# A planner's clock with other prices: transfers at 280 bytes per ns, table loads left out

## The chip, the cores and the metric

The kernel runs on one core of a Trainium2 chip. The metric is the device time of one execution in microseconds (us), less is better. Before the change three runs took 842.88, 843.17 and 847.2 us, a median of 843.17 us. Five engines work beside each other, each through its own queue in the order in which the program gave it the instructions: TensorE (PE, matrix products and transposes), VectorE (DVE), ScalarE (ACT), GpSimd (POOL) and SyncE (SP, which only issues DMA transfers here).

## The reference

Two layers of an encoder over 256 tokens of width 1024, all in fp32:

```python
h = rms_norm(x, norm_mix_g)
rq, rk, rv, rg, pv, nq, nk, nv, mq = split(h @ w_in, 9)      # each 256 wide
ret  = rms_norm(retention(rotary(rq), rotary(rk), rv)) * silu(rg)
pool = multiscale_pool(pv, pool_w, pool_scale)               # windows 2, 4, 8, 16
na   = neighbourhood_attention(norm(nq), norm(nk), nv, rpb)
mk, mv = split(rms_norm(mem, norm_mem_g) @ w_mem_kv, 2)      # 256 memory tokens
mo   = memory_attention(norm(mq), norm(mk), mv)
up   = einsum('bsnc,ncd->bsnd', stack([ret, pool, na, mo]), w_branch)
x    = x + sum(sigmoid(h @ w_gate) * up) @ w_out
a, g = split(rms_norm(x, norm_ffn_g) @ w_ffn_in, 2)          # 2816 wide each
x    = x + (silu(a) * g) @ w_ffn_out
```

Every branch has 4 heads of 64. The weights are 136 MB of the two layers together, read once.

## The kernel before, in words

**Weights.** The 256 tokens are two tiles `t` of 128. All weights pass through 272 slots of 128x1024 fp32 (512 KB), in a fixed order: 136 slots a layer (0 to 135, 136 to 271). A slot comes by DMA into one of four buffers `raw`; ACT copies it, rounded, to one of ten buffers `whi` (`split_hi`, a CAST in the profile); DVE subtracts that from `raw` into one of ten `wlo` (`split_lo`) and then issues the next transfer (`issue_dmas`). The two together are called the casts of a slot. TensorE multiplies with both halves: three products for each fp32 product (`whi` by the high half of the activation, `wlo` by its high half, `whi` by its low half), 12 matmuls of 512 columns a slot, into the PSUM banks A0 to A3 or B0, B1. Slots 0 to 17 of a layer are `w_in`; then come, branch by branch, the gates, the memory's keys and values (slots 22 to 25) and the branch projections; 62 to 69 are `w_out`, 70 to 135 the FFN.

**Small work.** Everything else is written as Python generators (chains): the evacuation of a bank, norms, softmax (`attention`, buffers `sc`), transposes through banks C0 and C1, retention, pooling (`branch_chain`), the FFN's hidden units (`hid_chain`, `hid_T`, buffers `w0` to `w3`), the gates (`gate_chain`, buffer `gt`).

**The planner.** No hand wrote the order on the queues. While the program is written out, a planning clock (`Clock`, L66) keeps a time for each engine and for the DMA: `enter` takes every instruction, `cost` prices it, and a tile's last write and read are noted with the time that comes out. All decisions ask `soon(t)`: is `t` at most a little past the time to which TensorE has been planned? `pump` puts the casts of the next slot into the ACT and DVE queues as soon as the clock says that the raw transfer has landed, the buffer is free and the engine's queue is not planned further ahead than `WINDOW` allows; `background` takes the next step of each chain that is due; the main loop then takes the next group of matmuls. So a price is never executed, but it decides which of two instructions stands first in a queue, and each engine then keeps that order on the chip whatever really lands first. A wrong price cannot give a wrong result: the semaphores follow from the order.

The transfer's price is in `enter`: SP is held 0.45 us, the data start 1.2 us after that at the earliest, pass at 390 bytes per ns (512 KB: 1.34 us) one after the other, and count as landed 1.0 us later. A switch of ACT's function table between exponential and sigmoid costs TABLE_LOAD. The instruction itself (ACT_TABLE_LOAD) is put in by the compiler wherever two activations that follow one another need different tables.

Of the kernel before, what the change touches and what calls it, by code (L numbers as in the profile page):

```python
# [9 lines left out]
F32 = mybir.dt.float32  # L10
F32R = mybir.dt.float32r
AF = mybir.ActivationFunctionType
# [11 lines left out]
HD = 64  # L24
# [9 lines left out]
LEAD = 7  # L34
MAX_LAG = 8
WARM = 6.6
TABLE_LOAD = 1.28
WINDOW = (6, 4, 1.5, 0.4)
VERBOSE = False
BRANCHES = (2, 3, 0, 1)  # L40
# [3 lines left out]
class Engine:  # L44


    def __init__(self, real, clock, name):
        self.real, self.clock, self.name = real, clock, name

    def __getattr__(self, op):  # L50
        f = getattr(self.real, op)

        def call(*args, **kw):
            outs = [kw[k] for k in ("out", "accum_out") if kw.get(k) is not None]
            ins = [v for k, v in kw.items() if k not in ("out", "accum_out")]
            rest = list(args)
            if "out" not in kw:
                outs.append(rest.pop(0))
            func = next((v for v in rest if isinstance(v, AF)), None)
            self.clock.enter(self.name, op, outs, [v for v in ins + rest if isinstance(v, bass.AP)], kw, func)  # L60
            return f(*args, **kw)  # L61

        return call


class Clock:  # L66
# [5 lines left out]
    def __init__(self):  # L72
        self.at = dict.fromkeys(("PE", "ACT", "DVE", "POOL", "SP", "DMA"), 0.6)
        self.reads, self.writes = {}, {}
        self.mark = 0.0
        self.column = None
        self.narrow = False
        self.table = None

    @property  # L80
    def now(self):
# [2 lines left out]
    def cost(self, eng, op, outs, ins, kw):  # L84
        n = max([x.free_size() for x in outs[-1:] + ins[:1]])
        if eng == "PE":
            o = outs[0]
            n = o.free_size() * (2 if self.now < WARM else 1)
            narrow = op == "matmul" and ins[0].dtype == F32 and o.partition_size() == HD
            change = 0.2 * (narrow != self.narrow)  # L90
            self.narrow = narrow
            if op == "transpose":
                return n * 0.845e-3 + change
            if ins[0].dtype == F32R:
                return n * 0.4167e-3 + 0.0135 + change
            half = o.partition_size() == HD and o.base_partition()
            if o.partition_size() == HD:
                pair, self.column = self.column, None if half else n
                if half and pair == n:
                    return 0.02  # L100
            return max(n, 128) * 1.67e-3 + change
        if eng == "ACT":
            return 0.1 + n * 0.83e-3 + 0.1 * (kw.get("accum_out") is not None) + 0.04 * isinstance(kw.get("scale"), bass.AP)
        if eng == "POOL":
            if op == "memset":
                return 0.1 + n * 1e-3
            return 0.3 + 0.17 * n
        if op in ("tensor_copy", "tensor_scalar", "tensor_scalar_mul", "tensor_scalar_add", "memset"):
            return 0.085 + n * 0.6e-3
        return 0.08 + n * 1.045e-3 + 0.05 * (op == "scalar_tensor_tensor")  # L110

    def span(self, x):
        (stride, parts), *free = x.ap
# [12 lines left out]
        old = [r for r in table.get(key, ()) if r[4] > end - 60 and not (p0 <= r[0] and r[1] <= p1 and lo <= r[2] and r[3] <= hi)]  # L126
        table[key] = old + [(p0, p1, lo, hi, end, eng)]

    def enter(self, eng, op, outs, ins, kw, func=None):
        ins = [x for x in ins if x.space != bass.MemoryType.DRAM]  # L130
        outs = [x for x in outs if x.space != bass.MemoryType.DRAM]
        skip = "PE" if eng == "PE" else None
        t = max([self.last(self.writes, x) + self.LATENCY for x in ins]
                + [self.last(self.reads, x, eng) + self.LATENCY for x in ins if x.space == bass.MemoryType.PSUM]
                + [max(self.last(self.writes, x, skip), self.last(self.reads, x, skip)) + self.LATENCY for x in outs] + [self.at[eng]])
        if func in (AF.Exp, AF.Sigmoid) and func != self.table:
            self.table = func
            self.at["ACT"] += TABLE_LOAD
            t = max(t, self.at["ACT"])
        if op == "dma_start":  # L140
            self.at[eng] = t + 0.45
            t = max(self.at["DMA"], t + 1.2) + (outs + ins)[0].nbytes() / 390e3
            self.at["DMA"] = t
            end = t + 1.0
        else:
            end = self.at[eng] = t + self.cost(eng, op, outs, ins, kw)
        for x in ins:
            self.note(self.reads, x, end, eng)
        for x in outs:
            self.note(self.writes, x, end, eng)  # L150
        self.mark = max(self.mark, end)
# [1030 lines left out]
```

## Time and profile before

| | |
|---|---|
| three runs | 842.88, 843.17, 847.2 us (median 843.17) |
| profiled execution | 841.89 us, its span 840.0 us |
| granted clock of TensorE | 1.000 of full speed (2.4 GHz) |
| PE busy | 820.8 us (98%), 3928 instructions |
| DVE, ACT busy | 552.2 us (66%), 470.1 us (56%) |
| DMA | 152.86 MB, mean 182 GB/s |
| chain that ended last | PE 78%, ACT 7%, DMA 7%, DVE 6%, issue 2% |

How to read it: all recorded instructions carry one line, L61, the helper through which every operation goes, so groups are told apart by the names of their tiles (written out<-in). Times in a timeline are microseconds from the start of the span. A timeline's row gives start, duration, engine, line, operation, tiles, shape, how many instructions it joins (x8), and in brackets how long the engine was idle before it and what released it. The end of a matmul is modelled: successive matmuls overlap, so the step from start to start is what a matmul costs.

### The profile page before, as it was taken

How to read it: one execution, taken by the hardware profiler on the slowest of the kernel's cores; microseconds unless marked ns; L12 is line 12 of the kernel's file. 1: busy time of each engine (PE TensorE's matmuls, PEld its weight loads, DVE VectorE, ACT ScalarE, POOL GpSimd, SP SyncE). 2: the span in 40 equal slices, each digit the busy share in tenths (PEclk: the TensorE clock that was granted, in tenths of full speed). 3: DMA queues.
4: the chain of work that ended last, by engine and by line, in shares of the span. 5: the costliest groups of instructions: out<-in, count | busy, mean ns of one | idle time of the engine just before them, and what ended most of it. 6: DMA issues, size and time to landing. Idle time of an engine off the chain costs nothing.

```text
span 840.0 us, 10795 instructions
## 1 busy us (share of the span) xinstructions
PE 820.8 (98%) x3928; PEld 672.4 (80%) x3928; DVE 552.2 (66%) x802; ACT 470.1 (56%) x726; POOL 30.5 (4%) x32
## 2 busy tenths in 40 slices
PE   8999999999999999999999998999999999999998
PEld 6788778778887888888888877887888878888886
DVE  5898786865677556555568868584775765655541
ACT  6858887445465444444469677754444654444430
POOL 0400100000000000000011001000000000000000
PEclk9999999999999999999999999999999999999999
DMA  8946765546568656566374477446544676666611
GB/s 257 323 140 203 240 199 166 166 147 197 176 180 255 191 180 197 176 198 185 95 220 137 156 246 219 147 126 226 178 157 120 200 228 198 187 187 186 189 52 51
DMA packets 103765, 152.86 MB, mean 182 GB/s; under 512 B 6432, under 2 KB 55328, under 8 KB 103712
## 3 DMA queue, kind: packets, MB, share of 16 engines
q1 hardware_dynamic: 102848, 151.30, 57.1%
q10 hardware_dynamic: 864, 0.88, 0.3%
q8 instruction: 31, 0.51, 0.2%
q14 instruction: 22, 0.18, 0.1%
HBM read 151.10 MB, written 1.05 MB: 181 GB/s over the span
## 4 chain that ended last, share of the span: by engine, by line
PE 78%; ACT 7%; DMA 7%; DVE 6%; issue 2%; POOL 0%; SPq 0%; DVEq 0%; ACTq 0%; POOLq 0%
PE A L61 49%; PE B L61 25%; PE C L61 4%; DVE wlo L61 3%; ACT whi L61 2%; DMA raw<-in_w_in 2%; DMA mem<-in_pool_a 2%; DMA raw<-in_w_ffn_out 1%; DMA raw<-in_w_gate 1%; DVE w L61 1%; ACT rs L61 1%; ACT sc L61 1%; DMA raw<-in_w_mem_kv 1%; ACT qk L61 1%; ACT bhi L61 1%
## 5 line engine op out<-in xcount | busy, mean ns | idle before, releaser
L61 DVE TENSOR_TENSOR wlo<-raw,whi 128x1024 fp32r<-128x1024 f32 (+1 forms) x275 | 330.2, 1212 | 190.9 <-ACT whi L61 190.3
L61 ACT CAST whi<-raw 128x1024 fp32r<-128x1024 f32 (+1 forms) x273 | 284.1, 1050 | 214.0 <-PE A L61 83.0
L61 PE MATMUL A<-whi,hhi 128*128 128x512 f32 (+1 forms) x544 | 213.9, 393 | 1.6 <-ACT whi L61 0.7
L61 PE MATMUL A<-wlo,hhi 128*128 128x512 f32 (+1 forms) x544 | 208.9, 384 | 1.0 <-DVE wlo L61 1.0
L61 PE MATMUL A<-whi,hlo 128*128 128x512 f32 (+1 forms) x544 | 209.1, 384 | 0.0
L61 PEld LDWEIGHTS A<-whi,hhi 128*128 128x128 f32 x544 | 102.3, 188 | 23.2 <-issue 2.6
L61 PEld LDWEIGHTS A<-whi,hlo 128*128 128x128 f32 x544 | 102.2, 188 | 21.2 <-DVE hlo L61 0.8
L61 PEld LDWEIGHTS A<-wlo,hhi 128*128 128x128 f32 x544 | 102.5, 188 | 20.1 <-DVE wlo L61 2.0
L61 PE MATMUL B<-whi,hlo 128*128 128x512 f32 x288 | 112.5, 391 | 0.1
L61 PE MATMUL B<-whi,hhi 128*128 128x512 f32 x288 | 112.3, 390 | 0.0
L61 PE MATMUL B<-wlo,hhi 128*128 128x512 f32 x288 | 112.1, 389 | 0.0
L61 PE MATMUL A<-whi,bhi 128*128 128x512 f32 x272 | 108.3, 398 | 0.0
L61 PE MATMUL A<-whi,blo 128*128 128x512 f32 x272 | 106.2, 390 | 0.0
L61 PE MATMUL A<-wlo,bhi 128*128 128x512 f32 x272 | 106.1, 390 | 0.0
L61 PEld LDWEIGHTS B<-whi,hlo 128*128 128x128 f32 x288 | 54.0, 188 | 12.9 <-DVE hlo L61 1.8
L61 PEld LDWEIGHTS B<-wlo,hhi 128*128 128x128 f32 x288 | 54.1, 188 | 11.3
L61 PEld LDWEIGHTS B<-whi,hhi 128*128 128x128 f32 x288 | 54.1, 188 | 11.0
L61 PEld LDWEIGHTS A<-whi,blo 128*128 128x128 f32 x272 | 51.1, 188 | 11.0
L61 PEld LDWEIGHTS A<-whi,bhi 128*128 128x128 f32 x272 | 51.1, 188 | 10.4 <-issue 0.8
L61 PEld LDWEIGHTS A<-wlo,bhi 128*128 128x128 f32 x272 | 51.2, 188 | 9.7
L61 DVE SCALAR_TENSOR_TENSOR w<-B,rms,w 128x256 f32<-128x256 f32 x72 | 34.7, 482 | 3.9 <-ACT w L61 2.6
L61 ACT CAST bhi<-C 128x512 fp32r<-128x512 f32 x28 | 16.4, 586 | 34.4 <-PE C L61 34.3
(115 smaller groups left out, 605.5 us busy)
## 6 DMA issues: line engine op xcount, KB each, us to landing
raw<-in_w_ffn_in SPq DMA_DIRECT2D x176, 256.0 KB, 3.2
raw<-in_w_gate SPq DMA_DIRECT2D x64, 512.0 KB, 4.4
raw<-in_w_ffn_out SPq DMA_DIRECT2D x44, 512.0 KB, 3.9
raw<-in_w_in SPq DMA_DIRECT2D x35, 512.0 KB, 4.3
raw<-in_w_branch SPq DMA_DIRECT2D x16, 512.0 KB, 4.5
raw<-in_w_out SPq DMA_DIRECT2D x16, 512.0 KB, 4.2
raw<-in_w_mem_kv SPq DMA_DIRECT2D x8, 512.0 KB, 4.3
xn<-in_bias SPq DMA_DIRECT2D x4, 512.0 KB, 5.4
```

Of the source, the lines that this page charges most:

```text
L61: return f(*args, **kw)
```

## The change

Only the prices of the planning clock change. Of a transfer: SP is held 0.48 us in place of 0.45, the data start 1.1 us later in place of 1.2, pass at 280 bytes per ns in place of 390 (512 KB: 1.87 us in place of 1.34), and count as landed 0.9 us later in place of 1.0. A switch of ACT's table costs the clock nothing any more (`TABLE_LOAD` and the `func` that was handed along are gone), nor does a change between matmuls of 64 and of 128 rows of output (`narrow`, 0.2 us). A transpose, an fp32r matmul (512 columns: 0.216 us in place of 0.227) and DVE's operations get slightly different prices.

```diff
-TABLE_LOAD = 1.28
...
-            narrow = op == "matmul" and ins[0].dtype == F32 and o.partition_size() == HD
-            change = 0.2 * (narrow != self.narrow)
-            self.narrow = narrow
             if op == "transpose":
-                return n * 0.845e-3 + change
+                return n * 0.84e-3
             if ins[0].dtype == F32R:
-                return n * 0.4167e-3 + 0.0135 + change
+                return n * 0.416e-3 + 0.003
...
-            return max(n, 128) * 1.67e-3 + change
+            return max(n, 128) * 1.67e-3
...
-            return 0.085 + n * 0.6e-3
-        return 0.08 + n * 1.045e-3 + 0.05 * (op == "scalar_tensor_tensor")
+            return 0.07 + n * 0.55e-3
+        return 0.07 + n * 1.05e-3 + 0.05 * (op == "scalar_tensor_tensor")
...
-        if func in (AF.Exp, AF.Sigmoid) and func != self.table:
-            self.table = func
-            self.at["ACT"] += TABLE_LOAD
-            t = max(t, self.at["ACT"])
         if op == "dma_start":
-            self.at[eng] = t + 0.45
-            t = max(self.at["DMA"], t + 1.2) + (outs + ins)[0].nbytes() / 390e3
+            self.at[eng] = t + 0.48
+            t = max(self.at["DMA"], t + 1.1) + (outs + ins)[0].nbytes() / 280e3
             self.at["DMA"] = t
-            end = t + 1.0
+            end = t + 0.9
```

The queues hold the same instructions as before, but for ACT_TABLE_LOAD: 12 in place of 10, both new ones in the second softmax of layer 0. Their order differs in the mixers (the part of a layer ahead of its FFN) of both layers and in the first blocks of each FFN; from the fourth block on the FFN's order is the same. On SP five raw transfers trade places with the bias, memory or norm tables beside them; on POOL one power in layer 0 moves ahead of two others. Both stay put otherwise, `pool_a` included.

The ACT queue in the first blocks of the FFN of layer 0, before (`whi` are casts of slots, `w3<-A2` the sigmoid of the first block's second tile, `bhi` the cast of transposed hidden units):

```order
L61 CAST whi5_78<-raw1_70 128x1024
L61 CAST whi6_79<-raw2_71 128x1024
L61 ACTIVATE w3_128<-A2_63,rms_136 128x256
L61 CAST whi7_80<-raw3_72 128x1024
L61 CAST whi8_81<-raw0_69 128x1024
L61 CAST bhi1_98<-C1_68 128x512
```

and now:

```order
L59 CAST bhi0_97<-C0_67 128x512
L59 CAST whi5_78<-raw1_70 128x1024
L59 ACTIVATE w3_128<-A2_63,rms_136 128x256
L59 CAST whi6_79<-raw2_71 128x1024
L59 CAST whi7_80<-raw3_72 128x1024
L59 CAST bhi1_98<-C1_68 128x512
```

The sigmoid stands ahead of the cast of slot 86 (`whi6`), where it stood behind it; the same trade is made in layer 1 with slot 222. In layer 1 the evacuation of the second tile of memory keys (`w3<-A2`) likewise moves ahead of the casts of slots 169 and 170, which stood ahead of it.

The ACT queue in the second softmax of layer 0, before (`sc0`, `sc1` with `sums` are exponentials, without it the scaling of their rows, `gt` the sigmoids of the first gates, `mem0` the retention's decay):

```order
L61 CAST whi5_78<-raw1_70 128x1024
L61 ACTIVATE sc0_119,sums0_151<-sc0_119,sums0_151 128x256 x2
L61 ACTIVATE sc1_120,sums1_152<-sc1_120,sums1_152 128x256 x2
L61 ACTIVATE mem0_123<-mem0_123 128x512
L61 ACTIVATE sc0_119<-sc0_119,sums0_151 128x256
L61 CAST whi6_79<-raw2_71 128x1024
L61 ACTIVATE sc1_120<-sc1_120,sums1_152 128x256
L61 ACT_TABLE_LOAD
L61 ACTIVATE gt_109<-A1_62,rms_136 128x512
L61 ACTIVATE gt_109<-A3_64,rms_136 128x512
L61 COPY sc0_119<-B0_65 128x512
L61 ACT_TABLE_LOAD
```

and now:

```order
L59 CAST whi5_78<-raw1_70 128x1024
L59 ACT_TABLE_LOAD
L59 ACTIVATE gt_109<-A1_62,rms_136 128x512
L59 CAST whi6_79<-raw2_71 128x1024
L59 ACT_TABLE_LOAD
L59 ACTIVATE sc0_119,sums0_151<-sc0_119,sums0_151 128x256 x2
L59 ACT_TABLE_LOAD
L59 ACTIVATE gt_109<-A3_64,rms_136 128x512
L59 ACT_TABLE_LOAD
L59 ACTIVATE sc1_120,sums1_152<-sc1_120,sums1_152 128x256 x2
L59 ACTIVATE mem0_123<-dist_150,lg_134 128x512
L59 ACTIVATE sc1_120<-sc1_120,sums1_152 128x256
```

The gates' sigmoids now stand between the exponentials, and a table load at every change from one to the other.

The TensorE queue in the pooling of layer 1, before (`B0<-mem0`, `mem1` are the pooling's products, whose `mem` tiles come by the transfer `pool_a`; the rows ahead are matmuls of slots 183 and 184):

```order
L61 MATMUL A3_64<-whi3_76,hhi1_94 128x512
L61 MATMUL A3_64<-wlo3_86,hhi1_94 128x512
L61 MATMUL A3_64<-whi3_76,hlo1_96 128x512
L61 MATMUL B0_65<-mem0_123,qk4_115 64x136 x2
L61 MATMUL B0_65<-mem0_123,qk4_115 64x16 x2
L61 MATMUL B0_65<-mem0_123,qk4_115 64x120 x2
L61 MATMUL B0_65<-mem1_124,qk4_115 64x136 x2
L61 MATMUL B0_65<-mem1_124,qk4_115 64x16 x2
L61 MATMUL B0_65<-mem1_124,qk4_115 64x120 x2
L61 MATMUL A1_62<-whi4_77,hhi0_93 128x512
L61 MATMUL A1_62<-wlo4_87,hhi0_93 128x512
L61 MATMUL A1_62<-whi4_77,hlo0_95 128x512
```

and now:

```order
L59 MATMUL A3_64<-whi4_77,hhi1_94 128x512
L59 MATMUL A3_64<-wlo4_87,hhi1_94 128x512
L59 MATMUL A3_64<-whi4_77,hlo1_96 128x512
L59 MATMUL A1_62<-whi5_78,hhi0_93 128x512
L59 MATMUL A1_62<-wlo5_88,hhi0_93 128x512
L59 MATMUL A1_62<-whi5_78,hlo0_95 128x512
L59 MATMUL B0_65<-mem0_123,qk4_115 64x136 x2
L59 MATMUL B0_65<-mem0_123,qk4_115 64x16 x2
L59 MATMUL B0_65<-mem0_123,qk4_115 64x120 x2
L59 MATMUL B0_65<-mem1_124,qk4_115 64x136 x2
L59 MATMUL B0_65<-mem1_124,qk4_115 64x16 x2
L59 MATMUL B0_65<-mem1_124,qk4_115 64x120 x2
```

The products stand 15 matmuls later, behind slot 184 and a quarter of slot 185; in layer 0 they stand 3 rows later than before.

## Rows read from the trace of the kernel before

**Rows 1.** The page's first part: busy time, share of the span and instructions by engine.

```profile
PE 820.8 (98%) x3928; PEld 672.4 (80%) x3928; DVE 552.2 (66%) x802; ACT 470.1 (56%) x726; POOL 30.5 (4%) x32
```

**Rows 2.** TensorE's waits: who waited for what, us in total, times, longest.

```profile
PE C L61 <- DVE w L61: 7.6, 5, 3.0
...
PE B L61 <- DMA mem<-in_pool_a: 1.8, 3, 1.1
```

**Rows 3.** Timeline of TensorE, layer 0 to 46 us and layer 1 from 440 us.

```profile
36.50 1.09 PE L61 MATMUL C<-ident_gain,w 128*128 128x128 f32 x8 [1.58 <-DVE blo L61]
...
45.69 0.66 PE L61 MATMUL C<-ident_gain,mem 128*128 128x128 f32 x4 [0.23 <-DVE blo L61]
...
440.65 0.39 PE L61 MATMUL A<-wlo,hhi 128*128 128x512 f32 x1
440.87 0.39 PE L61 MATMUL A<-whi,hlo 128*128 128x512 f32 x1
441.41 0.66 PE L61 MATMUL C<-ident_gain,mem 128*128 128x128 f32 x4
...
470.52 0.50 PE L61 MATMUL A<-wlo,hhi 128*128 128x512 f32 x1 [0.52 <-DVE wlo L61]
```

**Rows 4.** Timeline of TensorE, its other waits.

```profile
100.08 0.30 PE L61 MATMUL C<-ident_gain,w 128*128 128x128 f32 x1 [1.32 <-DVE w L61]
...
113.61 0.50 PE L61 MATMUL A<-whi,hhi 128*128 128x512 f32 x1 [0.64 <-DVE xn L61]
...
263.01 0.55 PE L61 MATMUL C<-ident_gain,w 128*128 128x128 f32 x3 [1.68 <-DVE w L61]
...
514.73 0.52 PE L61 MATMUL C<-ident_gain,w 128*128 128x128 f32 x3 [2.99 <-DVE w L61]
...
582.63 0.78 PE L61 MATMUL B<-mem,qk 128*64 128x136 f32 x12 [1.08 <-DMA mem<-in_pool_a]
...
676.94 0.55 PE L61 MATMUL C<-ident_gain,w 128*128 128x128 f32 x3 [0.96 <-DVE w L61]
```

**Rows 5.** Timeline of ACT and VectorE at the first FFN block of each layer.

```profile
259.74 1.05 ACT L61 CAST whi<-raw 128x1024 fp32r<-128x1024 f32 x1 [1.66 <-DMA raw<-in_w_ffn_out]
...
261.96 1.00 DVE L61 SCALAR_TENSOR_TENSOR w<-A,rms,w 128x256 f32<-128x256 f32 x2
...
673.66 1.05 ACT L61 CAST whi<-raw 128x1024 fp32r<-128x1024 f32 x1 [0.76 <-DMA raw<-in_w_ffn_out]
```

**Rows 6.** Timeline of ACT and GpSimd at the memory keys of layer 1.

```profile
505.56 1.05 ACT L61 CAST whi<-raw 128x1024 fp32r<-128x1024 f32 x1 [1.63 <-PE A L61]
...
507.24 1.05 ACT L61 CAST whi<-raw 128x1024 fp32r<-128x1024 f32 x1
...
509.02 0.49 ACT L61 ACTIVATE w<-A,rms 128x256 f32<-128x256 f32 x1
...
511.93 1.86 POOL L61 TENSOR_TENSOR sm<-sm,mhalf 128x4 f32<-128x4 f32 x1 [1.50 <-DVE sm L61]
```

**Rows 7.** Issue of the pooling tables in layer 1, and their time to landing.

```profile
576.01 0.82 SPq L61 DMA_DIRECT2D mem<-in_pool_a  x2
...
DMA to landing us min/median/max: 6.6/7.0/7.4
```

**Rows 8.** Timeline of ACT and TensorE at the second softmax of layer 0.

```profile
79.84 0.50 ACT L61 ACTIVATE sc<-sc,sums 128x256 f32<-128x256 f32 x1
80.36 1.28 ACT L61 ACT_TABLE_LOAD   x1
81.66 1.27 ACT L61 ACTIVATE gt<-A,rms 128x512 f32<-128x512 f32 x2
...
81.99 0.60 PE L61 MATMUL B<-ident_gain,sc 128*128 128x128 f32 x4
```

**Rows 9.** Timeline of VectorE and TensorE at slots 14 and 15 of layer 0.

```profile
52.31 2.35 DVE L61 TENSOR_TENSOR wlo<-raw,whi 128x1024 fp32r<-128x1024 f32 x2
...
54.39 0.39 PE L61 MATMUL A<-wlo,hhi 128*128 128x512 f32 x1
```

More of the change, by code (lines that the diff above doesn't have):

```diff
@@ L58, in call @@
                 outs.append(rest.pop(0))
-            func = next((v for v in rest if isinstance(v, AF)), None)
-            self.clock.enter(self.name, op, outs, [v for v in ins + rest if isinstance(v, bass.AP)], kw, func)
+            self.clock.enter(self.name, op, outs, [v for v in ins + rest if isinstance(v, bass.AP)], kw)
             return f(*args, **kw)
@@ L76, in __init__ @@
         self.column = None
-        self.narrow = False
-        self.table = None
     @property
@@ L127, in note, with enter @@
         table[key] = old + [(p0, p1, lo, hi, end, eng)]
-    def enter(self, eng, op, outs, ins, kw, func=None):
+    def enter(self, eng, op, outs, ins, kw):
         ins = [x for x in ins if x.space != bass.MemoryType.DRAM]
```

## The prediction

> **What bounds the kernel now.** I read the page's first part, then TensorE's waits, then each wait in the timeline with the queues it hangs on. TensorE is busy 820.8 of 840 us [rows 1], so the change can win little more than its waits. The table of waits shows where most are: 7.6 us in five waits of bank C for a `w` tile that VectorE writes, and 1.8 us in three waits for the pooling's tables [rows 2]. The timeline shows that all sit where small work (softmax, norms, hidden units) hands something to TensorE, none in the FFN's middle [rows 3, 4].
>
> A wait costs slightly more than its bracket says. A matmul of 512 columns is shown 0.39 us long, but the next starts 0.22 us after it [rows 3]; so a pause is the bracket plus some 0.16 us of refill. The wait before 36.50 costs 1.58 + 0.16 = 1.74, that at 514.73 costs 2.99 + 0.16 = 3.15. Where no bracket is shown, the step says it: from 440.87 to 441.41 is 0.54, of which 0.23 is the matmul and 0.31 a pause [rows 3].
>
> **What the change does.** It changes the order alone. With a slower transfer the clock believes that raw weights land later, so `pump` offers a cast later and small work gets ahead of it. That cuts both ways: small work comes sooner where a cast stood before it, and the cast comes later where its slot was just in time. No matmul, cast or byte is added; of instructions only two table loads, 1.28 us each on ACT [rows 8]. The slightly shorter prices of TensorE and VectorE bring no term of their own; what they do is in the order already. Terms, from the order as it now stands and durations of the trace:
>
> 1. **FFN starts.** The sigmoid of the first block's second tile stands ahead of the cast it stood behind. That cast waited for its transfer, ACT idle 1.66 us before 259.74 and 0.76 before 673.66 [rows 5], then took 1.05. VectorE could multiply only at 261.96, and TensorE's transposes stood until 263.01. In the new order the sigmoid doesn't wait for a landing, and with 2.7 us and 1.8 us gained (idle plus cast) both waits are gone: (1.68 + 0.16) + (0.96 + 0.16) = **-2.96** [rows 4, 5]. The cast that now stands later has its matmuls some slots away; its cover is the ring of ten buffers. Bounds: -2.96, and 0 if VectorE is late for another reason.
>
> 2. **Memory keys of layer 1.** The evacuation at 509.02 stood behind two casts, at 505.56 and 507.24, each some 0.95 from start to start; ACT was idle 1.63 before the first [rows 6]. Both go behind it: 1.9 sooner, and I count 0.4 of the idle time, as the first tile's evacuation is still ahead. The power on GpSimd, 1.86 us each [rows 6], remains, and the chain over it. The wait of 3.15 [rows 4] falls by **-2.3**. Bounds: 0 (the first power is late and holds the second) and -3.15.
>
> 3. **Pooling.** SP issues the tables at 576.01 and they land 6.6 to 7.4 us later [rows 7]; their place among the transfers is unchanged. The products that wait for them move 15 matmuls later in layer 1, 15 x 0.227 = 3.4 us of other work, against a wait of 1.08 + 0.16 and a smaller one behind it; in layer 0 by three rows, 0.7 us against its one. The three waits sum to 1.8 + 3 x 0.16 = 2.3 [rows 2, 4]: **-2.3**. What is late next is the pooled branch's projection, which the planner gives a slot's distance. Bounds: -2.3, and 0 if the transfer itself slips as far as the products, since its neighbours on SP are raw transfers that wait for casts.
>
> 4. **Gate products at 113.61**, held by VectorE's merging: 0.64 + 0.16 = **-0.8** [rows 4]; the sums now stand ahead of a cast. Bounds: -0.8 and 0.
>
> 5. **Start of layer 1**: 0.31 at 441.41 and 0.52 + 0.16 at 470.52 [rows 3]. The latter is a slot whose `wlo` is just late. Small work around it is reordered and the slot before it comes in sooner: **-1.0**. Bounds: -1.0, and +2.0 if more small work stands before that cast.
>
> 6. **Layer 0 up to 66 us.** Two waits go: 1.74 and 0.23 + 0.16, together -2.1 [rows 3]. But here weights are just in time: the first of the two subtractions from 52.31 (2.35 for both, so it ends near 53.5) is used at 54.39, a slack of 0.9 [rows 9]. Walking VectorE's new queue with the durations of the rows I find a cast about 1.0 late behind small work, and five small delays of 0.15 to 0.45 at banks and scores, together about 1.2. Net **+0.1**. Bounds: -2.1 (none of the new ones comes) and +3 (twice the new ones, rounded up).
>
> 7. **Second softmax of layer 0.** Now both exponentials run before any sigmoid; the scaling of `sc1` is done at 79.84 + 0.5, and its transposes stand in TensorE's queue at 81.99 without a wait [rows 8]. In the new order two gates (1.27) and four table loads stand ahead of it, where no load stood. A load steps 1.30 us from start to start, 80.36 to 81.66 [rows 8]: 4 x 1.30 + 1.27 = 6.5, so the scaling ends at 86.8 at the earliest. The transposes move 12 matmuls later, 2.7 us, to 85.0 with what changes around them: 1.9 late, and about 0.75 more since the casts ahead stand later too. I take 2.65, as casts there already wait for transfers. The two waits for memory keys at 100 us, 7.6 - 1.68 - 2.99 - 0.96 = 2.0 and 0.3 of refill [rows 2, 4], shrink by 1.0, since their cover on VectorE and GpSimd runs on while TensorE stands. Net **+1.65**. Bounds: -2.3 (no new wait, the old ones gone) and +4 (a cast more ahead, the old waits unchanged).
>
> That ACT row also bears on a page's rule. The exponential's scaling ended at 80.34, the load began at 80.36 and the next activation followed at once [rows 8], so a switch is seen to cost 1.30. The Trainium skill, "ScalarE: Activation LUTs", section "What ACT_TABLE_LOAD costs", gives 1283 ns for the load and some 1380 ns of draining beside it, 2.66 us a switch; its load agrees with the row, the drain is not in it, and by the page term 7 would be larger by four drains, an estimate of 5.5 us. The row decides.
>
> **Sum:** -2.96 - 2.3 - 2.3 - 0.8 - 1.0 + 0.1 + 1.65 = -7.6. The profiled execution took 841.89 us: 834.3. The median of the runs, 843.17, is 1.28 above it, so against the runs I say **835.6 us**, 0.9% less. A measurement of this kernel can tell about 0.5%, 4.2 us, from no change.
>
> **Rivals.**
>
> *The waits only change place* (0.22). For it: the planner packs the same work, and what ACT does sooner, GpSimd's power or a transfer can hold. Then half of terms 1 to 5 is real, -4.7, and terms 6 and 7 come as +0.1 and +1.65: -3, 840.2 us. Against it: terms 1 and 4 rest on rows in which one instruction plainly stands before the other.
>
> *The table loads cost more than their row* (0.05). If each load also held ACT for about as long again before or after it, four of them would add 4 x 1.3 = 5.2 us to the wait of term 7: -7.6 + 5.2 = -2.4, 840.8 us. For it: four loads in a row occur nowhere in the trace before. Against it: rows 8. The page named above states such a drain.
>
> *Weights starve* (0.12), the other side. Where the slot is just in time, small work before the subtraction goes straight to TensorE. Slots 14 to 18 of layer 0 (slack 0.9 [rows 9]) and 151 to 153 of layer 1 (one is 0.5 late already [rows 3]) are such places. If each of these eight slots gets 2.0 us of small work ahead, the price is about 1.1 for each of the five and 2 for each of the three, less what the ring gives back in between, in all some +9; term 5 is then lost, term 6 without its +0.1, and the other gains hold by half: -4.2 + 1.65 + 9 = +6.5, 849.7 us. It decides from about 1 us of small work before each of those casts. Against it: the planner still checks that TensorE's slot is near (`WINDOW`), and the new order puts such work before only some of them.
>
> That the change does not do what it says, casts behind small work everywhere, is true in part: the FFN's middle keeps its order, and a few casts move forward. That is in the sum.
>
> **How the numbers follow.** The forecast has 0.61 and lies below 839.0, the bound of faster; the first two rivals, 0.27, lie within 0.5%; the third, 0.12, above 847.4. The range reaches down to 831.0 (term 6 at its low end and half of term 7's) and up to 843.0, which takes in the two middle rivals and leaves out the starved case and a few in a hundred below. Chances: faster 0.61, same 0.27, slower 0.12.
>
> **What would show it.** In the profile after: twelve ACT_TABLE_LOAD; waits of C for `w` down from 7.6 to 2 or 3 us, with none near 260 and 674; no wait for the pooling's tables; a new wait of B near 85 us of 2 to 3 us, released by ACT's `sc`; a wait for `wlo` before 66 us. I am wrong if waits of A for `whi` or `wlo` pass some 4 us in sum, if the wait at 515 stays over 2 us, or if the pooling's products still wait for their tables.

## The result and the profile after

The changed kernel took 831.13 to 832.37 us in four runs, median 831.98, beside 843.64 of the kernel before: ratio 0.9857, interval 0.9834 to 0.988, so 11.7 us (1.4%) faster. The forecast was 835.6, its range 831.0 to 843.0.

The profiled executions stand 840.0 (before) to 829.9 us (span after), 10.1 less. TensorE's work is the same, 3928 instructions; its share is now 99% [rows 1]:

```profile
span 829.9 us, 10785 instructions
...
PE 819.2 (99%) x3928; PEld 672.9 (81%) x3928; DVE 552.8 (67%) x805; ACT 472.2 (57%) x725; POOL 29.4 (4%) x32
...
PE 87%; ACT 5%; DVE 4%; DMA 3%; issue 1%; POOL 1%; SPq 0%; DVEq 0%; ACTq 0%; POOLq 0%
```

In the chain that ended last TensorE has 87% in place of 78%, and DMA 3% in place of 7%. TensorE's waits after (who for what: us, times, longest):

```profile
PE B L59 <- ACT sc L59: 1.8, 1, 1.8
PE C L59 <- DVE w L59: 1.5, 2, 0.8
PE A L59 <- DVE wlo L59: 1.2, 3, 0.8
PE B L59 <- DVE mhalf L59: 1.0, 1, 1.0
PE A L59 <- ACT whi L59: 0.5, 1, 0.5
PE A L59 <- ACT hhi L59: 0.2, 1, 0.2
PE C L59 <- DVE blo L59: 0.2, 1, 0.2
```

The five waits of C for `w` fell from 7.6 to two of 1.5 in sum, those for the pooling's tables are gone [rows 2], and the first line is new: `sc`, behind the table loads. I walked all of TensorE's starts in both traces and counted each step above the matmul's own (0.227 us for 512 columns). Depending on the step counted as a matmul's own, these pauses sum to 28 to 30 us before and 18 to 20 after. The difference, 9.4 to 10.1 us, is nearly the whole gain of the profiled execution.

Where they stand after, in TensorE's timeline:

```profile
50.18 0.66 PE L59 MATMUL C<-ident_gain,mem 128*128 128x128 f32 x4 [0.24 <-DVE blo L59]
...
59.01 0.39 PE L59 MATMUL A<-wlo,hhi 128*128 128x256 f32 x1 [0.76 <-DVE wlo L59]
...
86.10 0.66 PE L59 MATMUL B<-ident_gain,sc 128*128 128x128 f32 x4 [1.79 <-ACT sc L59]
...
100.30 0.52 PE L59 MATMUL C<-ident_gain,w 128*128 128x128 f32 x3 [0.65 <-DVE w L59]
...
507.62 0.52 PE L59 MATMUL C<-ident_gain,w 128*128 128x128 f32 x3 [0.82 <-DVE w L59]
```

What the slower planned transfer does is seen on ACT: its idle time in front of casts that stood first in the queue and had not landed. Before:

```profile
ACT whi L61 <- DMA raw<-in_w_ffn_in: 5.1, 6, 1.3
ACT whi L61 <- DMA raw<-in_w_out: 4.8, 2, 3.3
ACT whi L61 <- DMA raw<-in_w_in: 4.5, 6, 1.9
ACT whi L61 <- DMA raw<-in_w_branch: 4.2, 2, 2.6
ACT whi L61 <- DMA raw<-in_w_mem_kv: 4.1, 5, 1.6
ACT whi L61 <- DMA raw<-in_w_gate: 3.8, 7, 1.0
ACT whi L61 <- DMA raw<-in_w_ffn_out: 2.4, 2, 1.7
```

And after:

```profile
ACT whi L59 <- DMA raw<-in_w_ffn_in: 6.1, 6, 1.7
ACT whi L59 <- DMA raw<-in_w_gate: 4.2, 7, 1.6
ACT whi L59 <- DMA raw<-in_w_branch: 3.0, 2, 1.8
ACT whi L59 <- DMA raw<-in_w_ffn_out: 1.6, 3, 1.1
ACT whi L59 <- DMA raw<-in_w_in: 1.6, 3, 0.8
ACT whi L59 <- DMA raw<-in_w_mem_kv: 1.1, 1, 1.1
```

28.9 us in 30 waits became 17.6 us in 22. The groups of the FFN change little in sum; what counts is what stands behind the waiting cast. At the first FFN start, after, the sigmoid runs at 255.95, and the cast behind it waits for its transfer as before [rows 5], but now TensorE does not wait behind it:

```profile
254.74 1.05 ACT L59 CAST whi<-raw 128x1024 fp32r<-128x1024 f32 x1 [0.29 <-DMA raw<-in_w_ffn_in]
255.95 0.48 ACT L59 ACTIVATE w<-A,rms 128x256 f32<-128x256 f32 x1
257.56 1.05 ACT L59 CAST whi<-raw 128x1024 fp32r<-128x1024 f32 x1 [1.13 <-DMA raw<-in_w_ffn_out]
```

TensorE's transposes of these hidden units, without a bracket (1.68 us before [rows 4]):

```profile
259.15 0.60 PE L59 MATMUL C<-ident_gain,w 128*128 128x128 f32 x4
```

### The profile page after: what moved, and what is told of

It is laid out like the page before. It is cut to its first block, busy times and chain, and to the rows that moved or that the text cites. A ratio compares the mean times of both kernels' runs of the same rounds, so it can differ in the third digit from the quotient of the medians.

```text
span 829.9 us, 10785 instructions
## 1 busy us (share of the span) xinstructions
PE 819.2 (99%) x3928; PEld 672.9 (81%) x3928; DVE 552.8 (67%) x805; ACT 472.2 (57%) x725; POOL 29.4 (4%) x32
## 4 chain that ended last, share of the span: by engine, by line
PE 87%; ACT 5%; DVE 4%; DMA 3%; issue 1%; POOL 1%; SPq 0%; DVEq 0%; ACTq 0%; POOLq 0%
PE A L59 57%; PE B L59 25%; PE C L59 4%; ACT whi L59 2%; DVE wlo L59 2%; DMA raw<-in_w_gate 1%; DVE w L59 1%; DMA raw<-in_w_ffn_in 1%; DMA raw<-in_w_in 1%; ACT L59 1%; DVE blo L59 1%; DMA raw<-in_w_mem_kv 1%; POOL sm L59 1%; ACT sc L59 0%; ACT rs L59 0%
```

## The experiments

Twelve kernels, each timed in turn with the kernel before, whose median beside them was 842.8 to 843.6. Intervals are of the ratio to it, 95%. Waits read from a timeline are given as the bracket or, where it says so, with the 0.16 us of refill.

### Which price does it

**The rate alone**, on the kernel before:

```diff
-            t = max(self.at["DMA"], t + 1.2) + (outs + ins)[0].nbytes() / 390e3
+            t = max(self.at["DMA"], t + 1.2) + (outs + ins)[0].nbytes() / 280e3
```

> The kernel before with one number changed: transfers planned at 280 bytes per ns; table loads, issue, start and landing times and all engine prices as they were. Its order: the sigmoid goes ahead of the cast at both FFN starts, the pooling's products of layer 1 stand 9 matmuls later (2.0 us), the memory keys of layer 1 stay behind their two casts, ten table loads. Theory (each changed order is worth the wait it ends, and most orders come from the rate): FFN starts -2.7, pooling -2.3, layer 0 up to 66 us -0.6, memory keys 0: -5.6 us, about 838. Rival (the other prices make the gain): within 2 us of the kernel before.

Measured: 833.18 us, ratio 0.9872 (0.985 to 0.9895), -10.3 us. The one number makes nearly all of the gain, more than I gave it. FFN starts (-2.7), pooling (-2.3) and layer 0 up to 66 us (-0.7) came as expected. Left out were three places that gained too, all with their refill: the memory keys of layer 0 at 100 us, 2.4 us before [rows 4] and 0.4 here; the gate products at 114 us, gone; and the memory keys of layer 1, 3.2 before [rows 4] and 2.0 here although their own order is unchanged.

**The other prices alone**, the changed kernel with 390:

```diff
-            t = max(self.at["DMA"], t + 1.1) + (outs + ins)[0].nbytes() / 280e3
+            t = max(self.at["DMA"], t + 1.1) + (outs + ins)[0].nbytes() / 390e3
```

> The changed kernel with transfers planned at 390 bytes per ns again, all its other prices kept. Its order: both FFN starts as before, one of the two casts ahead of the memory keys of layer 1 gone, the pooling's products 3 matmuls later (0.7 us of about 2), twelve table loads. Theory: memory keys -1.0, pooling -0.7, start of layer 1 -1.0, second softmax of layer 0 +0.4: -2.3 us, about 841. Rival (the other prices make the gain): -8 us or more, 835 or less.

Measured: 840.56 us, ratio 0.9959 (0.9939 to 0.998), -3.0 us: the theory's size. The rival falls. That the size fits is in part luck, for its profile does not hold the theory's terms: the pooling's waits are gone altogether (2.3 us with refill, not 0.7), and so is the wait at the first FFN start (1.8), although the order there is the old one; against that, the second softmax brings a wait of 2.2 us (0.4 in the theory) and the memory keys of layer 1 gain 0.4 in place of 1.0. On top of the rate, the other prices make 833.2 - 832.0 = 1.2 us between the medians; the two intervals overlap, so this much is not shown.

### Single waits, by hand

For these the kernel before keeps its prices and thus almost its whole order; `pump` skips the casts of the slots in `held_back` until the named activation has been put into the queue.

```diff
+    held_back = {86, 222}
...
+            if state["hi"] in held_back:
+                j = state["lo"]
+                if j < state["hi"] and soon(clock.at["DVE"], window) and soon(clock.last(clock.writes, WHI[j % NS])):
+                    split_lo()
+                break
...
         nc.scalar.activation(s, ps[:, :256], AF.Sigmoid, scale=RF[t])
+        if j == 1 and t == 1:
+            held_back.discard(86 + 136 * l)
```

> The kernel before with all its prices, and one rule by hand: the casts of slots 86 and 222 are put into the queue only behind the sigmoid of the second hidden block's second tile. Some ten rows a queue change places, nothing else. Theory: the waits of 1.84 and 1.12 us at 263 and 677 us end, 0.1 to 0.2 is left: -2.8 us, about 840.8, and those two waits are gone from the profile. Rival (a wait only changes place, the next transfer or the later cast takes it up): 0 to -1 us.

Measured: 839.77 us, ratio 0.9957 (0.9933 to 0.998), -3.7 us, and neither wait is in the profile. The interval runs from 1.7 to 5.7 us: it holds the theory's 2.8 and leaves out the rival. Two instructions that changed places are worth what their rows said.

**Memory keys of layer 1** in the same way, with `held_back = {169, 170}`, emptied behind the square of the second tile's keys:

> The kernel before with all its prices, and one rule by hand: in layer 1 the casts of slots 169 and 170 are put into the queue only behind the evacuation of the second tile of memory keys. The rest of that mixer shifts a little (the pooling's products 12 matmuls later), nothing before it or in the FFN changes. Theory: the wait of 3.16 us at 515 falls to about 1 and the pooling's 1.9 go too: -4.1 us, about 839.5. Rival (GpSimd's powers set the keys' end whatever stands ahead on ACT): the wait at 515 stays over 2.5 us, and only the pooling's 1.9 go, 841.7.

Measured: 840.08 us, ratio 0.9953 (0.9929 to 0.9976), -2.7 us. The wait at 515 is gone altogether, so term 2 has its cause: what stood ahead on ACT. The rival, that GpSimd sets the keys' end, falls. TensorE's waits of C for `w` are 3.8 in place of 7.6 [rows 2]:

```profile
PE C L61 <- DVE w L61: 3.8, 3, 1.7
...
PE C L61 <- ACT whi L61: 1.4, 1, 1.4
```

The pooling's waits are gone from this profile too. The interval, 2.0 to 6.0 us, still holds the theory's 4.1.

**Pooling**, products planned later:

```diff
             nc.sync.dma_start(out=MEM[r], in_=a["pool_a"][r])
-        yield
+        yield 3.4
```

> The kernel before with all its prices, and one rule by hand: the pooling's products are planned 3.4 us after the issue of their tables. They stand 15 matmuls later in both layers, and little else moves. Theory: the three waits for the tables (2.3 us) go and nothing new comes: -2.3 us, about 841.3. Rival (the work behind the pooling, its small product and the branch's projection, is late next): 0 to -1 us, and a new wait of A or B behind the pooling.

Measured: 842.90 us beside 842.78, ratio 0.9989 (0.9969 to 1.0008): no gain that can be told. The interval, from 2.6 us less to 0.7 more, holds the rival's size and, at its edge, the theory's 2.3 too, so the run does not decide between them. All three waits for the tables are gone from the profile, and there is no new wait right behind the pooling, where the rival put it. But the wait at the FFN start of layer 1 is 2.05 us with its refill where it was 1.12, and the granted clock fell to 0.50 right behind it. Why the FFN start is later here can't be said from one profile.

### The table loads

The second softmax of layer 0 on ACT, after:

```profile
75.30 1.28 ACT L59 ACT_TABLE_LOAD   x1
76.60 0.69 ACT L59 ACTIVATE gt<-A,rms 128x512 f32<-128x512 f32 x1
77.19 1.05 ACT L59 CAST whi<-raw 128x1024 fp32r<-128x1024 f32 x1
78.25 1.28 ACT L59 ACT_TABLE_LOAD   x1
79.55 0.51 ACT L59 ACTIVATE sc<-sc,sums 128x256 f32<-128x256 f32 x1
...
80.66 1.28 ACT L59 ACT_TABLE_LOAD   x1
81.96 0.69 ACT L59 ACTIVATE gt<-A,rms 128x512 f32<-128x512 f32 x1
82.65 1.28 ACT L59 ACT_TABLE_LOAD   x1
83.95 0.51 ACT L59 ACTIVATE sc<-sc,sums 128x256 f32<-128x256 f32 x1
...
85.56 0.49 ACT L59 ACTIVATE sc<-sc,sums 128x256 f32<-128x256 f32 x1
```

Each of the four loads steps 1.30 us to the next activation and begins within 0.02 us of the end of what stood before it. By the Trainium skill, "ScalarE: Activation LUTs", section "What ACT_TABLE_LOAD costs", a switch is the load (1283 ns) and a drain of some 1380 ns; the load agrees (1.28 us), and no drain is seen in any of the four.

**The gates held back** behind the second softmax's exponentials, on the changed kernel:

```diff
+            if r == 1:
+                raise_flag(f"soft{branch}@{l}")
...
-    def gate_chain(ps, g, t):
+    def gate_chain(ps, g, t, *after):
         yield
+        yield from need(*after)
```

> The changed kernel with one rule by hand: in layer 0 the first gates' sigmoids wait until the second softmax has its exponentials. Ten table loads in place of twelve, the rest of the order nearly the same. Theory: the wait of 1.96 us for the scaled scores at 86 us goes, but the memory keys at 100 us get back about half of what they had lost (1.5): -1.2 us, about 830.8. Rival (the keys' chain over GpSimd sets the end of that stretch): within 0.3 us of the changed kernel, 832, with the wait back at 100 us.

Measured: 830.44 us (829.69 to 832.19), ratio 0.9845 (0.9822 to 0.9869). The wait at 86 us is gone, that for the keys at 100 us rose from 0.8 to 1.1. It is 1.5 us below the changed kernel, near the 1.2 of the theory, but the two intervals overlap; it is the fastest median of all.

**Their price put back** (1.28 us for a switch), on the changed kernel:

> The changed kernel with a switch of ACT's table priced at 1.28 us again. The planner does not avoid them: sixteen table loads in place of twelve, four of them at the fourth softmax of layer 0; the scaled scores of the second softmax come a cast sooner and their transposes 9 matmuls later. Theory (a load costs only where TensorE waits behind it): the wait at 86 us goes and none of that size comes, 830 to 832. Rival (each added load is 1.3 us on the way): 832 + 4 x 1.3 = 837.

Measured: 836.36 us, ratio 0.9912 (0.9881 to 0.9942), 4.4 above the changed kernel. The theory is wrong: the wait at 86 us went, but a new one of 2.2 us stands at 143 us and one of 1.0 us right behind it, and the granted clock fell to 0.50 there. The rival's time is near, but its mechanism, 1.3 us for each added load, is not what the rows show: the evacuation that TensorE waits for (`bhi`) stood behind three casts and two gates, with one load ahead of them. How much of the wait that load makes was not tested.

```profile
136.28 1.28 ACT L60 ACT_TABLE_LOAD   x1
...
139.67 2.96 ACT L60 CAST whi<-raw 128x1024 fp32r<-128x1024 f32 x3
142.51 0.61 ACT L60 CAST bhi<-C 128x512 fp32r<-128x512 f32 x1
```

### How far the rate can go

Each is the changed kernel with another number in place of 280e3.

> The changed kernel with transfers planned at 330 bytes per ns in place of 280. Its order: the sigmoid stands behind the cast at both FFN starts as in the kernel before, one of two casts gone ahead of the memory keys of layer 1, the pooling's products 6 matmuls later, ten table loads. Theory (each order is worth the wait it ends): all of the changed kernel's gain but the FFN starts (2.7), 1 us of the memory keys, and without its 2 us behind the table loads: about -8.5 us, 835. Rival (the gain grows evenly with the rate's step, 60 of 110): -6.4 us, 837.

Measured: 833.31 us, ratio 0.9869 (0.9832 to 0.9907). I had misread its order: the sigmoids stand ahead of the casts here too. Without that mistake the theory says 835 - 2.7 = 832.3, near the result. The rival, that the gain grows evenly, falls.

> The changed kernel with transfers planned at 240 bytes per ns. Its order: as the changed kernel at the FFN starts and memory keys, the pooling's products 27 matmuls later still, twelve table loads with all four of the second softmax of layer 0 one cast sooner and its transposes 3 matmuls later. Theory (no wait of the changed kernel is longer here, that at 86 us is shorter): 830 to 832. Rival (weights begin to starve): waits for whi and wlo over 4 us in sum and 835 or more.

Measured: 834.61 us, ratio 0.9886 (0.9852 to 0.9919). The theory was wrong, and the rival is near: five waits for `wlo` sum to 3.0 us, all before 66 us, where weights are just in time, and one for `whi` is 1.2.

> The changed kernel with transfers planned at 160 bytes per ns, far below what they reach. All small work stands several casts sooner, sixteen table loads. Theory (casts have 5 us of cover in most places and less than 3 at the start of a layer): TensorE waits for whi or wlo, 10 us or more in sum, 840 or more. Rival (the casts' cover takes it up): waits for whi and wlo stay under 3 us, 832 or less.

Measured: 904.3 us, ratio 1.0718 (1.0682 to 1.0755), 61 us slower than before. The theory holds, and starving (TensorE waiting for weights) is much dearer than its lower bounds:

```profile
PE A L59 <- DVE wlo L59: 17.5, 23, 2.0
PE A L59 <- ACT whi L59: 11.8, 7, 2.5
```

One such place on ACT, at the pooling of layer 0:

```profile
187.76 0.58 ACT L59 COPY w<-B 128x512 f32<-128x512 f32 x1 [7.22 <-PE B L59]
189.53 0.47 ACT L59 ACTIVATE bhi<-B,cols 128x256 fp32r<-128x256 f32 x1 [1.18 <-PE B L59]
190.56 0.47 ACT L59 ACTIVATE bhi<-B,cols 128x256 fp32r<-128x256 f32 x1 [0.55 <-DVE blo L59]
190.93 1.98 ACT L59 CAST whi<-raw 128x1024 fp32r<-128x1024 f32 x2
```

ACT sits idle for 7.22 us before a copy whose products TensorE has not yet made, with a cast behind it in the queue whose transfer had landed at 178.0; TensorE then stands 2.5 us for that `whi`. It is the mirror of what was wrong before: there casts that had not landed stood before ready small work, here small work that is not ready stands before landed casts. With the other prices of the change the medians by planned rate are 840.6 (390), 833.3 (330), 832.0 (280), 834.6 (240) and 904.3 (160): within 2.6 us from 330 to 240, and far off at 160; between 240 and 160 nothing was run.

### Does a wait cost more than its length

Multiplications by 1.0 of one tile of hidden units, put on VectorE ahead of the transposes of blocks 4, 6 and 8 of each layer of the changed kernel, three in one kernel and twelve in the other:

```diff
         yield from acquire(c)
+        for _ in range(3 if j in (4, 6, 8) else 0):
+            nc.vector.tensor_scalar_mul(HID[j % 2][0][:, 1, :], HID[j % 2][0][:, 1, :], 1.0)
```

> The changed kernel with three multiplications by 1.0 (0.3 us each) put into VectorE's queue ahead of the transposes of the hidden units of blocks 4, 6 and 8 of each layer: six waits of TensorE of 0.5 to 1 us added. Theory (a wait of TensorE of 2 us or more also lowers its granted clock for some us, a shorter one doesn't): longer by the sum of the six waits in the profile, 3 to 6 us, and a granted clock of 0.998 or more. Rival (waits of any length lower it): more than the waits, clock under 0.995.

Measured: 838.76 us, 6.8 above the changed kernel. Six waits of 1.06 us with their refill make 6.4, and the mean clock is 0.998 to 1.000 in six executions: as the theory has it for short waits. The rival falls.

> As the kernel with short waits, but twelve multiplications in each place: six waits of 3 to 3.5 us. Theory (a wait of 2 us or more lowers the granted clock for some us): longer than the changed kernel by the waits' sum of about 20 us and by 4 to 10 us more, a mean clock of 0.985 to 0.993, and slow stretches right behind the waits. Rival (a wait costs its length, the drops seen elsewhere have another cause): longer by the waits' sum alone, clock 0.998 or more.

Measured: 867.34 us, 35.4 above the changed kernel; six waits of 4.02 us make 24.1, and 11.3 us come on top, at a mean clock of 0.982 to 0.986. Behind the second of them, TensorE's timeline and then the granted clock by stretches (start:end, length, busy time of PE, PEld, DVE, ACT, POOL with counts, clock, DMA share, GB/s):

```profile
341.27 1.11 PE L59 MATMUL C<-ident_gain,w 128*128 128x128 f32 x4 [3.86 <-DVE w L59]
342.04 0.78 PE L59 MATMUL A<-whi,bhi 128*128 128x512 f32 x1
342.61 0.63 PE L59 MATMUL A<-wlo,bhi 128*128 128x512 f32 x1
343.04 0.63 PE L59 MATMUL A<-whi,blo 128*128 128x512 f32 x1
```

```profile
330.00:337.00 7.00, 7.00 (x32) 5.82 (x31) 5.05 (x7) 3.29 (x5) 0.00 (x0) 1.00 0.70 207
341.00:344.00 3.00, 2.73 (x9) 2.34 (x10) 0.92 (x3) 1.53 (x2) 0.00 (x0) 0.50 0.00 1
```

The clock is granted at 0.50 of 2.4 GHz, its 1.2 GHz level, right behind the wait, and a matmul then steps 0.43 us in place of 0.23. The trace shows the same at all six waits: the lower level begins inside four of them and up to 1.5 us behind the end of the other two. TensorE's steps in these six stretches are together 12.0 us longer than the same steps at full clock, which makes up the 11.3 us. So these waits did lower the clock, and the rival falls; the theory's sizes (20 and 4 to 10 us) were a little low.

The theory's limit of 2 us is not shown. The two kernels test 1.06 and 4.02 us only. Elsewhere the clock fell behind waits of 1.89, 1.85 and 2.37 us (FFN starts by hand) and just after one of 1.44 us (memory keys by hand), and it stayed at full speed behind 2.99 us (the kernel before, [rows 4]) and 2.13 us (the rate of 330). The length of a wait alone does not tell.

## Why the prediction was right

Direction, mechanism and most terms held; the gain was 11.7 us where 7.6 was forecast. Of the 11.7, 9.2 lie in the seven terms, 0.9 in small pauses, and the other 1.6, as argued below, in the granted clock. By its own steps, each from the pauses of the two profiles (bracket and refill):

| term | forecast | measured | |
|---|---|---|---|
| 1 FFN starts | -2.96 | -2.73 | both waits gone, 0.23 left at 667 us; shown alone (the block is the second, j = 1, not the first as the text has it) |
| 2 keys of layer 1 | -2.3 | -2.18 | 3.16 to 0.98; shown alone |
| 3 pooling | -2.3 | -2.32 | gone here; alone no gain that can be told |
| 4 gate products | -0.8 | -0.80 | gone |
| 5 start of layer 1 | -1.0 | -0.98 | three waits of 1.28 gone, one more than the two that were counted; a new one of 0.30 |
| 6 layer 0 to 66 us | +0.1 | -0.63 | mis-sized |
| 7 second softmax | +1.65 | +0.42 | mis-sized |
| sum | -7.6 | -9.2 | of 10.1 in the profiled execution |

**Term 6** counted 2.2 us of new waits; 1.1 came: 0.92 at 59 us for the `wlo` of slot 16, as foreseen, and 0.18 at 49 us. Of the two waits that were to go, only the first went. The small one at 45.69 [rows 3] stands at 50.18 as long as before.

**Term 7** had the mechanism right and two sizes wrong. The wait behind the loads is 1.96 us with its refill and not 2.65: "about 0.75 more since the casts ahead stand later too" failed. The scaled scores were ready at 85.56 + 0.49 = 86.05, sooner than the 86.8 that was worked out as the earliest, by about as much as the layer was ahead by then (0.6 us, term 6). The 1.9 without that addition was right. And the waits at 100 us shrank by 1.5, not by 1.0.

**Not in the sum** are 0.9 us in small pauses, which I had not itemized, and the clock. The sum was made against a profiled execution at a granted clock of 1.000, and I carried the 1.28 us between it and the median over as a constant. It isn't one. 53 executions of the kernel before have a mean clock of 0.996 and a median of 843.4 us; the six of them at 1.000 have a median of 841.6. The four of the changed kernel stand at 0.998 to 1.000. Where the clock falls is seen in the profile of the FFN starts by hand: behind the waits at 37, 102 and 515 us, the first of which the changed kernel ends and the other two shortens to under 1 us. That a clock fall costs time is shown; that its absence makes the whole 1.6 us here is argued from these numbers.

**Luck.** The measured 832.0 lies only 1.0 us inside the range's lower end. That end was drawn from terms 6 and 7 alone, so the time fell inside the range without the clock having been foreseen. Of the signs named beforehand all came, two of them smaller than said: waits of C for `w` of 1.5 us, and a wait of B near 86 us of 1.79.

**The rivals.** That the waits only change place is refuted for the whole; for the pooling alone it is open. The table loads cost their row. Starving was on the right track in its mechanism and place: slot 16 waits 0.92 us here, and at 240 all waits for `wlo` lie before 66 us. But the point from which it decides lies beyond this change's 280: there, waits for `whi` and `wlo` sum to 1.7 us.

What stays open: whether ending the pooling's waits alone brings anything, what the other prices add to the rate, and how the gain of the gates held back stands to the changed kernel within a few tenths of a per cent.

## What to carry to other kernels

In a kernel whose order comes from a planner, the price of a transfer sets who stands first in a queue, and being wrong costs on both sides: priced too cheap, the engine stands idle before what has not landed while ready work queues behind it; priced too dear, landed weights queue behind small work. Look for idle time of the evacuating engine that a DMA ends, and read what stands next in that queue: that instruction's waiting consumer is the price. When summing waits, don't treat the gap between a profiled execution and the median as fixed: compare granted clocks first.

## What the runs showed that was not expected

A wait of TensorE can cost more than it lasts. Six waits of 1.06 us left the granted clock at 0.998 or more; six of 4.02 us brought it to 0.982 to 0.986, with 0.50 of full speed granted in or right behind every one of them, and cost 11.3 us beside their 24.1. The spread of the kernel before goes with the clock: at a mean of 1.000 it took 840.0 to 842.1 us, at 0.991 846.8 to 848.5. It does not hold for each execution: at 0.997 it took 841.3 to 845.7. The changed kernel, whose longest wait is 1.79 us, stayed within 1.3 us in four runs.
